# Strassen's form for 15 of 22 gate/up pairs of the first four feed-forward layers

## The chip, the cores and the metric

The kernel runs on one core of one Trainium2 chip. TensorE (PE) multiplies matrices, VectorE (DVE) and ScalarE (ACT) work on tiles elementwise, GpSimd (POOL) does elementwise work and issues some DMAs, SyncE (SP) issues most DMAs. SBUF and PSUM are the memories on the core. The metric is the device time of one execution in microseconds (us), lower being better: 3693.38 us, the median of three runs (3691.35 to 3710.01).

## The reference

One sequence of 512 tokens of width 1024, in float32, goes through two stacks of two layers each. The first stack, for each of its two layers, is

```
x = layer_norm(alpha * x + 0.5 * swiglu_ffn(x, ffn1_wi[l], ffn1_wo[l]), ...)
x = layer_norm(alpha * x + mixer(x), ...)          # even_mixer, then odd_mixer
x = layer_norm(alpha * x + 0.5 * swiglu_ffn(x, ffn2_wi[l], ffn2_wo[l]), ...)

def swiglu_ffn(x, wi, wo):                          # wi 1024 x 5632, wo 2816 x 1024
    gate, up = jnp.split(x @ wi, 2, axis=-1)
    return (jax.nn.silu(gate) * up) @ wo
```

These four `swiglu_ffn` are the feed-forward layers that the change touches. The mixers are a gated linear recurrence, an mLSTM, an RWKV and a gated linear attention. The second stack has two layers of three attention branches, each followed by a feed-forward layer with a convolution; the change leaves them alone.

## The kernel before

**Products in three parts.** Activations lie transposed, with the features in the 128 partitions and the 512 tokens in the free dimension. A float32 operand is split into a high part in float32r (`AF.Copy` to that type, on ACT) and a low part, the operand minus its high part (on DVE). `mm3` (L389) issues three matmuls for one 128 x 128 weight block: weight high by activation high, weight high by activation low, weight low by activation high. Each loads its weights anew.

**Weights.** `plan_w` lists every weight slab of the program in the order of use. A gate or up slab has 8 blocks of 128 rows by 128 columns and comes as two raw tiles `wr` of 128 x 512 (256 KB each), loaded by SP. `_split_hi` makes the high parts `wh`, `_split_lo` the low parts `wl`. `slab()` splits the slab that is now used, if that has not happened yet, and then lets `split_ahead` split `ahead` slabs more (1 in these layers), as long as no more than `hl_bufs` = 8 slabs are split and not done; `slab_done` ends a slab. `raw_bufs` = 3 slabs are loaded ahead of the splitting.

**One feed-forward layer** (`ffn_block1`, L730). The 22 blocks of 128 hidden features are done in `PARTS` of 6, 8 and 8. Each block j is a pair: a gate tile (8 blocks, 24 matmuls) and an up tile. `unit` then makes silu(gate) * 0.5 * up (`sg` on ACT, `hf` on DVE) and splits it (`hh` on ACT, `hl` on DVE). After each part, eight tiles of `wo` (`down`, `gemm_tile`) add the part to `ys`; the last part does this in `out_proj_ln`. The first two pairs of a layer are done by `gemm_first` (L555), which holds four slabs at once and loops over the eight blocks k outermost, since the layer norm before it delivers the activations block by block; in three of the four layers it does this for the two halves of the tokens one after the other. At every second k (of the second half, or of the only pass) it calls `split_ahead`. After it, eight sums `y` = `xh` + `xl` restore the activations on DVE, and pair 2 follows.

**A layer's end.** `out_proj_ln` (L685) holds its four last slabs at once and does them for each half of the tokens; the layer norm of the first half (`ln_half`, DVE and ACT) runs beside the second half's matmuls. The next stage begins with its own `gemm_first` on four slabs.

**Order.** A planner of the kernel's own (`Sched`) keeps an estimate of each engine's time while the program is written and decides where background work, such as the layer norm, stands between the main work's instructions. The framework then schedules these instructions and gives tiles their buffers; all tiles named by `g.f` share 90 buffers. DVE, ACT and POOL take their queues in order. The profile puts nearly all instructions on a helper's line (L55, L279), so tiles tell them apart: `mf` is the PSUM tile of `gemm_first`, `m` of `gemm_tile`, `mg` of `gemm_group`, `mh` of the last four slabs.

Of the kernel before, what the change touches and what calls it, by code (L numbers as in the profile page):

```python
# [12 lines left out]
F32R = mybir.dt.float32r  # L13
# [209 lines left out]
        assert not self.blocked  # L223


class G:


    def __init__(self, ctx, tc, raw_bufs=3, hl_bufs=8, f_bufs=90, q_bufs=16):
        self.s = Sched()  # L230
        self.ctx, self.tc, self.nc = ctx, tc, Core(tc.nc, self.s)
        pool = lambda name, bufs=1, **kw: ctx.enter_context(tc.tile_pool(name=name, bufs=bufs, **kw))
        self.const = pool("const")
        self.fp = pool("fp", f_bufs)
        self.qp = pool("qp", q_bufs)
        self.qsp = pool("qsp", 24)
        self.dram = pool("dram", 1, space=bass.MemoryType.DRAM)
        self.psp = pool("psp", 8, space=PSUM)
        self.raw_bufs, self.hl_bufs, self.ahead = raw_bufs, hl_bufs, 1
        self.wq = []  # L240
# [90 lines left out]
    def plan_w(self, w, c0, cols, k0, kt):  # L331

        src = w[k0 * P:(k0 + kt) * P, c0:c0 + cols].rearrange("(k p) c -> p k c", p=P)
        self.plan(lambda t, k, n: self.nc.sync.dma_start(t, src[:, k:k + n]), kt, cols)

    def _dma(self):
        while self.wi_dma < len(self.wq) and self.wi_dma < self.wi_split + self.raw_bufs:
            load, kt, cols = self.wq[self.wi_dma]
            per = NT // cols
            self.whl_t[self.wi_dma] = parts = []  # L340
            for k0 in range(0, kt, per):
                n = min(per, kt - k0)
                t = self.f("wr", F32, n * cols)
                load(t.rearrange("p (k c) -> p k c", c=cols), k0, n)
                parts.append(t)
            self.wi_dma += 1

    def split_ahead(self, n=1):

        self._dma()  # L350
        while n > 0 and self.wi_split < min(len(self.wq), self.wi_done + self.hl_bufs):
            self._split()
            n -= 1

    def _split_hi(self):
        parts = []
        for t in self.whl_t[self.wi_hi]:
            hi = self.f("wh", F32R, t.shape[1])
            self.nc.scalar.activation(hi, t, AF.Copy)
            parts.append((t, hi))  # L360
        self.whl_t[self.wi_hi] = parts
        self.wi_hi += 1

    def _split_lo(self):
        j = self.wi_split
        cols = self.wq[j][2]
        hl = []
        for raw, hi in self.whl_t[j]:
            lo = self.f("wl", F32R, raw.shape[1])
            self.nc.vector.tensor_tensor(lo, raw, hi, ALU.subtract)  # L370
            for k in range(lo.shape[1] // cols):
                c = slice(k * cols, (k + 1) * cols)
                hl.append((hi[:, c], lo[:, c]))
        self.whl_t[j] = hl
        self.wi_split += 1
        self._dma()

    def _split(self):

        if self.wi_hi == self.wi_split:  # L380
            self._split_hi()
        if self.wi_hi == self.wi_split + 1 and self.wi_hi < min(len(self.wq), self.wi_done + self.hl_bufs):
# [67 lines left out]
HALF = (slice(0, 256), slice(256, 512))  # L450
ALPHA = 4.0 ** 0.25
PARTS = ((0, 6), (6, 8), (14, 8))


class Pipe:
# [260 lines left out]
        g.s.spawn(finish(hf))  # L716


def plan_ffn(g, w_a, w_b, hook=None):
    for k0, n in PARTS:  # L720
        for j in range(k0, k0 + n):
            g.plan_w(w_a, j * P, P, 0, KD)
            g.plan_w(w_a, 2816 + j * P, P, 0, KD)
        for m in range(KD):
            g.plan_w(w_b, m * P, P, k0, n)
        if hook and k0 == 0:
            hook()


def ffn_block1(g, xs, gv, bv, hook=None, into=None, by_half=True):  # L730

    nc = g.nc
    ys = [g.f("y") for _ in range(KD)]
    st = Stats(g, True)
    pipe = Pipe()
    for pi, (k0, n) in enumerate(PARTS):
        hs = {}

        def unit(j, pg, pu):
            sg, hf = g.f("sg"), g.f("hf")  # L740
            nc.scalar.activation(sg, pg(), AF.Silu)
            g.rel()
            yield True
            nc.vector.scalar_tensor_tensor(hf, sg, 0.5, pu(), ALU.mult, ALU.mult)
            g.rel()
            hh, hl = g.f("hh", F32R), g.f("hl", F32R)
            nc.scalar.activation(hh, hf, AF.Copy)
            yield True
            nc.vector.tensor_tensor(hl, hf, hh, ALU.subtract)
            hs[j] = (hh, hl)  # L750

        j = k0
# [1899 lines left out]
def kernel(ctx: ExitStack, tc: tile.TileContext, d, out: bass.AP):  # L2652
# [25 lines left out]
    plan_ffn(g, d["ffn1_wi"][0], d["ffn1_wo"][0])  # L2678
    plan_even(g, d["ev_w_in"][0], d["ev_w_out"][0])
    plan_ffn(g, d["ffn2_wi"][0], d["ffn2_wo"][0])  # L2680
    plan_ffn(g, d["ffn1_wi"][1], d["ffn1_wo"][1])
    plan_odd(g, d["od_w_in"][0], d["od_w_out"][0], lambda l: plan_mem(g, d["w_mem_kv_2"][l]))
    plan_ffn(g, d["ffn2_wi"][1], d["ffn2_wo"][1])
    for l in range(2):
        plan_attn(g, d, l)
        plan_ffn2(g, d, l)
# [9 lines left out]
        return tc.manual_schedule(engines=e) if e != set() else contextlib.nullcontext()  # L2696

    with man("f"):
        x = ffn_block1(g, x0, *ln(0, 0), hook=lambda: g.s.spawn(first_setups()), by_half=False)
    with man("even"):  # L2700
        x = even_block(g, x, d, *ln(0, 1))
    with man("f"):
        x = ffn_block1(g, x, *ln(0, 2))
        x = ffn_block1(g, x, *ln(1, 0), hook=lambda: setup_odd(g, d))
# [50 lines left out]
```

## Time and profile before

| | us |
|---|---|
| median of 3 runs | 3693.38 (3691.35 to 3710.01) |
| the profiled execution | 3691.82 |
| its span, first to last instruction | 3689.6 |
| PE busy | 3633.5 (98%), 19704 matmuls |
| DVE busy | 2062.8 (56%) |
| ACT busy | 1460.8 (40%) |
| POOL busy | 359.2 (10%) |

The mean granted TensorE clock is 0.989 of full speed. The span holds the four changed layers at about 16 to 390, 610 to 990, 990 to 1360 and 1770 to 2140 us. An instruction's row shows its start, its duration and, in brackets, how long its engine was idle before it and what ended that; rows that are merged have a count (x2). Durations of neighbours on one engine overlap, so the distance of starts is what one costs in a dense queue.

### The profile page before, as it was taken

To read this page: it belongs to the slowest core of one execution; us is meant where nothing else is said; L and a number is where in the kernel's file an instruction comes from. 1 tells how busy PE (TensorE), PEld (TensorE's weight loads), DVE (VectorE), ACT (ScalarE), POOL (GpSimd) and SP (SyncE) were. 2 spreads that over 40 slices of the span, in tenths; PEclk is the share of its full clock that TensorE was granted. 3 is DMA by queue.
4 is the path that set the end of the run, shared out by engine and by line. 5 is a ranking of instruction groups with operands and counts; after the bars stand their busy time and mean duration, and the time that the engine had idled before them with its cause. 6 is when DMAs were issued, how large, how long until landed. Compare 5 with 4: busy or idle time off the path is not lost.

```text
span 3689.6 us, 52324 instructions
## 1 busy us (share of the span) xinstructions
PE 3633.5 (98%) x19704; PEld 2982.4 (81%) x19704; DVE 2062.8 (56%) x3771; ACT 1460.8 (40%) x2837; POOL 359.2 (10%) x547
## 2 busy tenths in 40 slices
PE   9999999999999999999999999999999999999999
PEld 7888878888888887677888888788888887888888
DVE  4333878432643266767633375557666745467755
ACT  4223664232333236534422353435333444354433
POOL 0001103000200021010100130022000300130001
PEclk9999999999999999989999999999999999999999
DMA  5333222332333221113233333332333332323231
GB/s 158 100 100 84 75 70 87 104 98 86 89 106 97 86 75 52 39 39 98 84 104 98 90 91 118 89 104 67 99 97 90 105 112 85 100 83 101 86 97 52
DMA packets 615087, 331.78 MB, mean 90 GB/s; under 512 B 25234, under 2 KB 608051, under 8 KB 614835
## 3 DMA queue, kind: packets, MB, share of 16 engines
q1 hardware_dynamic: 612018, 324.81, 30.3%
q10 hardware_dynamic: 2816, 3.64, 0.3%
q8 instruction: 154, 2.52, 0.3%
q14 instruction: 99, 0.80, 0.1%
HBM read 323.65 MB, written 4.74 MB: 89 GB/s over the span
## 4 chain that ended last, share of the span: by engine, by line
PE 91%; DVE 6%; ACT 1%; issue 1%; POOL 0%; DMA 0%; SPq 0%; DVEq 0%; POOLq 0%; ACTq 0%
PE m L279 64%; PE mg L279 5%; PE mf L279 4%; PE mh L279 4%; PE tk L279 3%; PE br L279 2%; DVE wl L55 1%; DVE ln_z L55 1%; DVE x L55 1%; DVE rm_t L55 1%; DVE rst L55 1%; PE st L279 1%; DVE xgl L55 0%; PE S L279 0%; PE mv L279 0%
## 5 line engine op out<-in xcount | busy, mean ns | idle before, releaser
L55 DVE TENSOR_TENSOR wl<-wr,wh 128x512 fp32r<-128x512 f32 (+2 forms) x1208 | 815.3, 720 | 114.9 <-ACT wh L55 114.4
L55 ACT ACTIVATE wh<-wr 128x512 fp32r<-128x512 f32 (+2 forms) x1208 | 663.9, 607 | 93.1 <-PE m L279 50.8
L279 PE MATMUL m<-xh,wh 128*128 128x512 f32 x1544 | 619.6, 401 | 0.0
L279 PE MATMUL m<-xh,wl 128*128 128x512 f32 x1544 | 610.9, 396 | 0.0
L279 PE MATMUL m<-xl,wh 128*128 128x512 f32 x1544 | 610.4, 395 | 0.0
L279 PE MATMUL m<-xgh,wh 128*128 128x512 f32 x1184 | 470.7, 398 | 0.0
L279 PE MATMUL m<-xgl,wh 128*128 128x512 f32 x1184 | 466.3, 394 | 0.0
L279 PE MATMUL m<-xgh,wl 128*128 128x512 f32 x1184 | 466.0, 394 | 0.0
L55 DVE SCALAR_TENSOR_TENSOR hf<-sg,m 128x512 f32<-128x512 f32 x80 | 55.0, 688 | 575.0 <-PE m L279 565.7
L279 PEld LDWEIGHTS m<-xh,wh 128*128 128x128 f32 x1544 | 291.0, 188 | 74.6 <-issue 7.3
L279 PEld LDWEIGHTS m<-xh,wl 128*128 128x128 f32 x1544 | 291.0, 188 | 69.1 <-issue 0.4
L279 PEld LDWEIGHTS m<-xl,wh 128*128 128x128 f32 x1544 | 291.2, 189 | 67.6 <-issue 1.7
L279 PEld LDWEIGHTS m<-xgh,wh 128*128 128x128 f32 x1184 | 222.3, 188 | 55.9 <-issue 5.3
L279 PEld LDWEIGHTS m<-xgh,wl 128*128 128x128 f32 x1184 | 222.3, 188 | 52.4
L279 PEld LDWEIGHTS m<-xgl,wh 128*128 128x128 f32 x1184 | 222.4, 188 | 49.9
L279 PE MATMUL m<-hh,wh 128*128 128x512 f32 x600 | 236.5, 394 | 0.0
L279 PE MATMUL m<-hl,wh 128*128 128x512 f32 x600 | 236.3, 394 | 0.0
L279 PE MATMUL m<-hh,wl 128*128 128x512 f32 x600 | 236.2, 394 | 0.0
L55 ACT ACTIVATE sg<-m 128x512 f32<-128x512 f32 x80 | 47.8, 598 | 424.1 <-PE m L279 424.1
L55 ACT ACTIVATE hh<-hf 128x512 fp32r<-128x512 f32 x88 | 55.7, 633 | 382.6 <-DVE hf L55 382.6
L55 ACT ACTIVATE uc<-up,vecs 128x512 f32<-128x512 f32 x88 | 71.7, 817 | 202.3 <-DVE up L55 202.3
L55 DVE SCALAR_TENSOR_TENSOR uc<-up,vecs,uc 128x512 f32<-128x512 f32 x176 | 131.3, 748 | 12.9 <-ACT uc L55 6.8
(546 smaller groups left out, 6330.3 us busy)
## 6 DMA issues: line engine op xcount, KB each, us to landing
wr<-in_ffn_wi_dram SPq DMA_DIRECT2D x352, 256.0 KB
wr<-in_w_up_dram SPq DMA_DIRECT2D x176, 256.0 KB
wr<-in_ffn_wo_dram SPq DMA_DIRECT2D x160, 256.0 KB
wr<-in_w_in_dram SPq DMA_DIRECT2D x152, 256.0 KB
wr<-in_w_down_dram SPq DMA_DIRECT2D x80, 256.0 KB
wr<-in_od_w_in_dram SPq DMA_DIRECT2D x50, 256.0 KB
wr<-in_ev_w_in_dram SPq DMA_DIRECT2D x48, 256.0 KB
wr<-in_w_out_dram SPq DMA_DIRECT2D x32, 256.0 KB
```

The lines of the kernel that those rows point to most:

```text
L55: r = fn(*a, **kw)
L279: return self.nc.tensor.matmul(out, lhsT, rhs, start=start, stop=stop, **kw)
```

## The change

Write the weights of one pair as a 2 x 2 block matrix: rows 1 and 2 are the two halves of the 1024 inputs, columns 1 and 2 are gate and up. The activations' blocks are the two halves of the inputs by the two halves of the tokens. Strassen's form (in Winograd's variant) computes gate and up with 7 block products instead of 8, of which each has 4 blocks k by 256 tokens. The names A11 to A22 are weight blocks of 128 x 512, S1 to S4 sums or differences of them, T1 to T4 those of the activations' blocks.

`FAST` names the 15 pairs that are done so: 3 to 7, 9, 10, 12 to 15, 17, 18, 20 and 21. `Combos` makes T1 to T4 and their high and low parts once per layer, spawned after the eight sums; a fast product waits for them. Each of the 7 products is a slab of one tile. Its factor is loaded or made on DVE, its high part is made on ACT; the low parts of S2 and S1 are made by a negated copy of the raw factor to float32r on ACT and a DMA from POOL's queue that adds the raw factor to it. The other five low parts are DVE's as before. `Fast.step` adds the products up, on DVE, as their PSUM banks become complete.

In the four layers, lookahead is now counted in tiles of 128 x 512: at most `RAW1` = 6 raw ones, and `HL0` = 9 (in `gemm_first` and from the last part's output on) or `HL1` = 7 (between) split and not done; `ahead` is 2.

```diff
+class Pair:
...
+    ORDER = ("A11", "S2", "A12", "S3", "S1", "A22", "S4")
+    BY_DMA = ("S2", "S1")
+    FETCH = {"A11": ("A11", "A21"), "S2": ("A22",), "A12": ("A12",)}
...
+    def factor(self, nm):
...
+        t, TT = self.t, self.g.nc.vector.tensor_tensor
+        if nm == "A11":
+            return t["A11"]
+        if nm == "S2":
+            t["S1"], t["S2"] = self.g.f("ws"), self.g.f("ws")
+            TT(t["S1"], t["A21"], t["A22"], ALU.add)
+            TT(t["S2"], t["S1"], t["A11"], ALU.subtract)
+            return t["S2"]
+        if nm == "S3":
+            TT(t["A21"], t.pop("A11"), t["A21"], ALU.subtract)
+            return t.pop("A21")
+        if nm == "S4":
+            TT(t["A12"], t["A12"], t.pop("S2"), ALU.subtract)
+            return t.pop("A12")
+        return t[nm] if nm == "A12" else t.pop(nm)
...
+    def room(self, i):
+        if i >= len(self.wq):
+            return False
+        if not self.raw_lim:
+            return i < self.wi_done + self.hl_bufs
+        return sum(1 if isinstance(load, Pair) else -(-kt * cols // NT)
+                   for load, kt, cols in self.wq[self.wi_done:i + 1]) <= self.hl_lim
+
     def split_ahead(self, n=1):
         self._dma()
-        while n > 0 and self.wi_split < min(len(self.wq), self.wi_done + self.hl_bufs):
+        while n > 0 and self.room(self.wi_split):
             self._split()
             n -= 1
...
             lo = self.f("wl", F32R, raw.shape[1])
-            self.nc.vector.tensor_tensor(lo, raw, hi, ALU.subtract)
+            if isinstance(self.wq[j][0], Pair) and self.wq[j][1] in Pair.BY_DMA:
+                self.nc.scalar.activation(lo, raw, AF.Copy, scale=-1.0)
+                self.nc.gpsimd.dma_start(lo, raw, accum_op=ALU.add)
+            else:
+                self.nc.vector.tensor_tensor(lo, raw, hi, ALU.subtract)
...
+FAST = tuple(j for j in range(3, 22) if j not in (8, 11, 16, 19))
+RAW1, HL0, HL1 = 6, 9, 7
...
+class Combos:
...
+    def make(self):
...
+        for k in range(4):
+            lo, hi = self.ys[k], self.ys[4 + k]
+            s, u = g.f("ta"), g.f("tb")
+            TT(s[:, a], lo[:, b], lo[:, a], ALU.subtract)
+            TT(s[:, b], hi[:, b], s[:, a], ALU.subtract)
+            yield g.pace()
+            TT(u[:, a], hi[:, b], lo[:, b], ALU.subtract)
+            TT(u[:, b], hi[:, a], s[:, b], ALU.subtract)
+            yield g.pace()
+            for nm, t in (("s", s), ("u", u)):
+                h, l = g.f("th", F32R), g.f("tl", F32R)
+                g.split_x(h, l, t)
...
+class Fast:
+    def product(self, nm):
...
+        w = g.slab()
+        for k in range(4):
+            x = self.cb(nm, k)
+            g.s.upto(*w[k], *x)
+            g.mm3(self.ps[bank][:, HALF[c]], w[k], x, k == 0, k == 3)
+        g.slab_done()
...
+    def step(self, nm):
...
+        self.product(nm)
...
+        if nm == "S2":
+            c = self.c1 = g.f("c1")
+            nc.scalar.copy(c[:, a], ps("a")[:, a])
+            TT(c[:, b], c[:, a], ps("a")[:, b], ALU.add)
...
+        elif nm == "S3":
+            u = self.c2 = g.f("c2")
...
+            TT(u[:, b], c[:, b], ps("b")[:, b], ALU.add)
+            TT(c[:, a], c[:, a], ps("b")[:, a], ALU.add)
...
+        elif nm == "A22":
...
+            TT(c[:, b], c[:, b], ps("d")[:, b], ALU.add)
...
+            TT(v(w), v(ps("d")), u[:, None, b].to_broadcast([P, 2, 256]), ALU.add)
...
+        elif nm == "S4":
+            c = self.c1
+            TT(c[:, b], c[:, b], ps("e")[:, a], ALU.add)
...
-def ffn_block1(g, xs, gv, bv, hook=None, into=None, by_half=True):
+def ffn_block1(g, xs, gv, bv, hook=None, into=None, by_half=True, fast=()):
     nc = g.nc
+    g.raw_lim, g.hl_lim, g.ahead = RAW1, HL0, 2
...
             for k in range(KD):
                 nc.vector.tensor_tensor(ys[k], xs.h[k], xs.l[k], ALU.add)
-        while j < k0 + n:
-            ps = [gemm_tile(g, xs)]
-            pipe.add(unit(j, lambda: ps[0], lambda: ps[1]))
-            ps.append(gemm_tile(g, xs))
-            pipe.step()
-            j += 1
+            g.hl_lim = HL1
+            cb = Combos(g, xs, ys)
+            if fast:
+                g.s.spawn(cb.make())
+        for j, nm in pair_order(range(j, k0 + n), fast):
+            if nm is None:
...
+            g.s.wait(lambda: cb.n == 4)
...
+            e.step(nm)
+            if nm == "S4":
+                pipe.add(unit_fast(j, e))
         pipe.drain()
+        if pi == len(PARTS) - 1:
+            g.hl_lim = HL0
...
+    g.raw_lim, g.ahead = 0, 1
     return xn[0]
```

## Rows read from the trace of the kernel before

**Rows 1.** The page: busy time of engines, and the chain by engine.
```profile
PE 3633.5 (98%) x19704; PEld 2982.4 (81%) x19704; DVE 2062.8 (56%) x3771; ACT 1460.8 (40%) x2837; POOL 359.2 (10%) x547
...
PE 91%; DVE 6%; ACT 1%; issue 1%; POOL 0%; DMA 0%; SPq 0%; DVEq 0%; POOLq 0%; ACTq 0%
```

**Rows 2.** The chain in order of time, whole span: start, us, engine, tile, line, count.
```profile
644.38 44.33 PE m L279 x191
697.04 114.10 PE m L279 x492
...
996.40 18.50 PE mf L279 x156
1014.90 44.50 PE m L279 x192
...
1794.94 44.55 PE m L279 x192
```

**Rows 3.** Groups by shape, PE's weight loads: busy us, mean ns, idle before.
```profile
L279 PEld LDWEIGHTS m<-xh,wh 128*128 128x128 f32 x1544 | 291.0, 188 | 74.6 <-issue 7.3
```

**Rows 4.** Timeline of DVE inside a pair of the first layer: start us, us.
```profile
151.94 1.29 DVE L55 TENSOR_TENSOR wl<-wr,wh 128x512 fp32r<-128x512 f32 x2
153.14 0.68 DVE L55 TENSOR_TENSOR hl<-hf,hh 128x512 fp32r<-128x512 f32 x1
153.74 1.29 DVE L55 TENSOR_TENSOR wl<-wr,wh 128x512 fp32r<-128x512 f32 x2
```

**Rows 5.** Groups by shape, DVE, whole span: a half-width operation on PSUM.
```profile
L55 DVE TENSOR_TENSOR y<-y,mh 128x256 f32<-128x256 f32 x48 | 19.9, 415 | 21.0 <-PE mh L279 21.0
```

**Rows 6.** Timeline of ACT inside a pair of the first layer.
```profile
130.39 1.14 ACT L55 ACTIVATE wh<-wr 128x512 fp32r<-128x512 f32 x2
```

**Rows 7.** Waits of PE: in total, times, longest, us.
```profile
PE xT L284 <- DMA xs<-in_x_dram: 7.9, 7, 3.7
```

**Rows 8.** Timeline of DVE after the third layer's `gemm_first`.
```profile
1015.85 0.69 DVE L55 SCALAR_TENSOR_TENSOR hf<-sg,mf 128x512 f32<-128x512 f32 x1 [3.40 <-ACT sg L55]
1017.23 0.69 DVE L55 TENSOR_TENSOR hl<-hf,hh 128x512 fp32r<-128x512 f32 x1 [0.70 <-ACT hh L55]
...
1018.44 4.90 DVE L55 TENSOR_TENSOR y<-xh,xl 128x512 f32<-128x512 f32 x8
1023.26 1.28 DVE L55 TENSOR_TENSOR wl<-wr,wh 128x512 fp32r<-128x512 f32 x2
```

**Rows 9.** Timeline of PE: first product of pair 2, first layer.
```profile
38.84 0.40 PE L279 MATMUL m<-xh,wh 128*128 128x512 f32 x1
```

**Rows 10.** Timeline of DVE: first wl behind the sums, layers 1, 2 and 4.
```profile
52.00 1.29 DVE L55 TENSOR_TENSOR wl<-wr,wh 128x512 fp32r<-128x512 f32 x2
...
651.40 1.29 DVE L55 TENSOR_TENSOR wl<-wr,wh 128x512 fp32r<-128x512 f32 x2
...
1802.39 1.29 DVE L55 TENSOR_TENSOR wl<-wr,wh 128x512 fp32r<-128x512 f32 x2
```

**Rows 11.** Timeline of DVE between the second and the third layer.
```profile
995.16 0.43 DVE L55 TENSOR_TENSOR sq<-sq,sqt 128x256 f32<-128x256 f32 x1
...
997.42 1.30 DVE L55 TENSOR_TENSOR wl<-wr,wh 128x512 fp32r<-128x512 f32 x2
998.63 0.42 DVE L55 TENSOR_TENSOR rst<-st_v,rs 128x256 f32<-128x256 f32 x1
```

**Rows 12.** Windows of 2 us: busy us of each engine, granted clock, DMA share, GB/s.
```profile
570.00:572.00 2.00, 1.42 (x7) 0.81 (x5) 2.00 (x2) 0.00 (x0) 2.00 (x3) 1.00 0.78 220
572.00:574.00 2.00, 0.28 (x1) 0.31 (x2) 1.49 (x4) 0.88 (x3) 2.00 (x3) 0.88 0.14 43
574.00:576.00 2.00, 2.00 (x6) 1.52 (x6) 0.78 (x3) 1.74 (x2) 0.46 (x2) 0.50 0.01 4
576.00:578.00 2.00, 2.00 (x11) 1.74 (x10) 1.72 (x3) 0.18 (x1) 0.00 (x0) 0.76 0.00 0
```

More of the change, by code (lines that the diff above doesn't have):

```diff
@@ L223, in drain, with __init__, fetch @@
         assert not self.blocked
+class Pair:
+    ORDER = ("A11", "S2", "A12", "S3", "S1", "A22", "S4")
+    BY_DMA = ("S2", "S1")
+    FETCH = {"A11": ("A11", "A21"), "S2": ("A22",), "A12": ("A12",)}
+    def __init__(self, g, w, c1, c2):
+        self.g, self.t = g, {}
+        self.src = {n: w[512 * (b - 1):512 * b, c:c + P].rearrange("(k p) c -> p k c", p=P)
+                    for n, b, c in (("A11", 1, c1), ("A12", 2, c1), ("A21", 1, c2), ("A22", 2, c2))}
+    def fetch(self, nm):
+        for n in self.FETCH.get(nm, ()):
+            t = self.t[n] = self.g.f("wr")
+            self.g.nc.sync.dma_start(t.rearrange("p (k c) -> p k c", c=P), self.src[n])
+    def factor(self, nm):
[14 more added lines that the diff above has]
+        return t[nm] if nm == "A12" else t.pop(nm)
 class G:
@@ L334, in plan_w, with raw_tiles @@
         self.plan(lambda t, k, n: self.nc.sync.dma_start(t, src[:, k:k + n]), kt, cols)
+    def raw_tiles(self, a, b):
+        n = 0
+        for load, kt, cols in self.wq[a:b]:
+            n += len(Pair.FETCH.get(kt, ())) if isinstance(load, Pair) else -(-kt * cols // NT)
+        return n
     def _dma(self):
-        while self.wi_dma < len(self.wq) and self.wi_dma < self.wi_split + self.raw_bufs:
+        while self.wi_dma < len(self.wq) and (
+                self.raw_tiles(self.wi_split, self.wi_dma) < self.raw_lim if self.raw_lim else
+                self.wi_dma < self.wi_split + self.raw_bufs):
             load, kt, cols = self.wq[self.wi_dma]
+            if isinstance(load, Pair):
+                load.fetch(kt)
+                self.whl_t[self.wi_dma] = None
+                self.wi_dma += 1
+                continue
             per = NT // cols
@@ L356, in _split_hi @@
         parts = []
+        load, nm, _ = self.wq[self.wi_hi]
+        if isinstance(load, Pair):
+            self.whl_t[self.wi_hi] = [load.factor(nm)]
         for t in self.whl_t[self.wi_hi]:
@@ L716, in out_proj_ln, with pair_order, plan_ffn @@
         g.s.spawn(finish(hf))
-def plan_ffn(g, w_a, w_b, hook=None):
-    for k0, n in PARTS:
-        for j in range(k0, k0 + n):
-            g.plan_w(w_a, j * P, P, 0, KD)
-            g.plan_w(w_a, 2816 + j * P, P, 0, KD)
+def pair_order(js, fast):
+    for j in js:
+        for nm in Pair.ORDER if j in fast else (None,):
+            yield j, nm
+def plan_ffn(g, w_a, w_b, hook=None, fast=()):
+    for k0, n in PARTS:
+        pairs = {}
+        for j, nm in pair_order(range(k0, k0 + n), fast):
+            if nm is None:
+                g.plan_w(w_a, j * P, P, 0, KD)
+                g.plan_w(w_a, 2816 + j * P, P, 0, KD)
+            else:
+                if j not in pairs:
+                    pairs[j] = Pair(g, w_a, j * P, 2816 + j * P)
+                g.plan(pairs[j], nm, P)
         for m in range(KD):
@@ L727, in plan_ffn, with __init__, __call__ @@
             hook()
-def ffn_block1(g, xs, gv, bv, hook=None, into=None, by_half=True):
+class Combos:
+    def __init__(self, g, xs, ys):
+        self.g, self.xs, self.ys = g, xs, ys
+        self.t = {}
+        self.n = 0
+    def make(self):
+        g = self.g
+        TT = g.nc.vector.tensor_tensor
+        a, b = HALF
+        for k in range(4):
[10 more added lines that the diff above has]
+                g.split_x(h, l, t)
+                self.t[nm, k] = (h, l)
+            self.n = k + 1
+            yield g.pace()
+        self.ys = None
+    PLACE = {"T1": ("s", 0), "T2": ("s", 1), "T3": ("u", 0), "T4": ("u", 1)}
+    OF = {"A11": "B11", "A12": "B21", "S4": "B22", "A22": "T4", "S1": "T1", "S2": "T2", "S3": "T3"}
+    def __call__(self, nm, k):
+        b = self.OF[nm]
+        if b[0] == "B":
+            return self.xs(k + 4 * (int(b[1]) - 1), HALF[int(b[2]) - 1])
+        o, q = self.PLACE[b]
+        h, l = self.t[o, k]
+        return h[:, HALF[q]], l[:, HALF[q]]
@@ new lines, with __init__ @@
+class Fast:
+    PLACE = {"A11": ("a", 0), "S2": ("a", 1), "A12": ("b", 0), "S3": ("b", 1), "S1": ("d", 1), "A22": ("d", 0),
+             "S4": ("e", 0)}
+    def __init__(self, g, cb):
+        self.g, self.cb = g, cb
+        self.ps = {}
+    def product(self, nm):
+        g = self.g
+        bank, c = self.PLACE[nm]
+        if bank not in self.ps:
+            g.acq_main(1)
+            self.ps[bank] = g.psum("m")
+        w = g.slab()
[4 more added lines that the diff above has]
+        g.slab_done()
+        g.s.pump()
+    def step(self, nm):
+        g, nc, TT = self.g, self.g.nc, self.g.nc.vector.tensor_tensor
+        self.product(nm)
+        ps = self.ps.get
+        a, b = HALF
+        if nm == "S2":
+            c = self.c1 = g.f("c1")
+            nc.scalar.copy(c[:, a], ps("a")[:, a])
+            TT(c[:, b], c[:, a], ps("a")[:, b], ALU.add)
+            del self.ps["a"]
+            g.rel()
+        elif nm == "S3":
[3 more added lines that the diff above has]
+            TT(c[:, a], c[:, a], ps("b")[:, a], ALU.add)
+            del self.ps["b"]
+            g.rel()
+        elif nm == "A22":
+            u, c = self.c2, self.c1
+            TT(c[:, b], c[:, b], ps("d")[:, b], ALU.add)
+            v = lambda t: t.rearrange("p (h n) -> p h n", h=2)
+            w = g.f("c2")
+            TT(v(w), v(ps("d")), u[:, None, b].to_broadcast([P, 2, 256]), ALU.add)
+            self.c2 = w
+            del self.ps["d"]
+            g.rel()
+        elif nm == "S4":
+            c = self.c1
+            TT(c[:, b], c[:, b], ps("e")[:, a], ALU.add)
+            del self.ps["e"]
+            g.rel()
@@ L750, in unit, with unit_fast @@
             hs[j] = (hh, hl)
+        def unit_fast(j, e):
+            sg, hf = e.c1, e.c2
+            nc.scalar.activation(sg, sg, AF.Silu)
+            yield True
+            nc.vector.scalar_tensor_tensor(hf, sg, 0.5, hf, ALU.mult, ALU.mult)
+            hh, hl = g.f("hh", F32R), g.f("hl", F32R)
+            nc.scalar.activation(hh, hf, AF.Copy)
+            yield True
+            nc.vector.tensor_tensor(hl, hf, hh, ALU.subtract)
+            hs[j] = (hh, hl)
         j = k0
@@ L760, in ffn_block1 @@
                 nc.vector.tensor_tensor(ys[k], xs.h[k], xs.l[k], ALU.add)
-        while j < k0 + n:
-            ps = [gemm_tile(g, xs)]
-            pipe.add(unit(j, lambda: ps[0], lambda: ps[1]))
-            ps.append(gemm_tile(g, xs))
-            pipe.step()
-            j += 1
+            g.hl_lim = HL1
+            cb = Combos(g, xs, ys)
+            if fast:
+                g.s.spawn(cb.make())
+        open_ = {}
+        for j, nm in pair_order(range(j, k0 + n), fast):
+            if nm is None:
+                ps = [gemm_tile(g, xs)]
+                pipe.add(unit(j, lambda: ps[0], lambda: ps[1]))
+                ps.append(gemm_tile(g, xs))
+                pipe.step()
+                continue
+            g.s.wait(lambda: cb.n == 4)
+            if j not in open_:
+                open_[j] = Fast(g, cb)
+            e = open_[j]
+            e.step(nm)
+            if nm == "S4":
+                pipe.add(unit_fast(j, e))
+                del open_[j]
         pipe.drain()
+        if pi == len(PARTS) - 1:
+            g.hl_lim = HL0
         of = lambda k, c=slice(0, NT): (hs[k0 + k][0][:, c], hs[k0 + k][1][:, c])
@@ L2702 @@
     with man("f"):
-        x = ffn_block1(g, x, *ln(0, 2))
-        x = ffn_block1(g, x, *ln(1, 0), hook=lambda: setup_odd(g, d))
+        x = ffn_block1(g, x, *ln(0, 2), fast=FAST)
+        x = ffn_block1(g, x, *ln(1, 0), hook=lambda: setup_odd(g, d), fast=FAST)
     mkv, mhl = [], ([], [])
@@ L2711 @@
         rx = ffn_block1(g, x, *ln(1, 2),
-                            into=lambda: RX(g, [g.f("x") for _ in range(KD)], v["g_pre_mix0"]))
+                            into=lambda: RX(g, [g.f("x") for _ in range(KD)], v["g_pre_mix0"]), fast=FAST)
     for l in range(2):
```

13 lines of the change are left out of this document (7 added, 6 removed).

## The prediction

> **What bounds the kernel now.** I read the page first: its first part gives TensorE (PE) 98% of the span and VectorE (DVE) 56%, and the chain that ended last is PE work for 91% [rows 1]. So time leaves only with PE work, or comes where PE is made to wait. The chain in order of time then gives both prices of a product. A stretch of 492 products, all with 512 moving columns (16 gate/up tiles of 24 and 6 down tiles of 18), takes 114.10 us: 0.2319 each. 156 products with 256 columns take 18.50 us: 0.1186 each [rows 2]. Halving the columns costs only 2% per column, though each product loads new weights.
>
> Last, I read the joints between stages, where the chain leaves PE, in the timelines of DVE and PE; their rows come with the parts below that use them.
>
> **Products removed.** An ordinary pair is 2 tiles x 8 k x 3 = 48 products: 48 x 0.2319 = 11.13 us. A fast pair is 7 block products x 4 k x 3 = 84 products of 256 columns: 84 x 0.1186 = 9.96 us. Four layers x 15 pairs x 1.17 us = **70 us saved**, all on PE's path.
>
> Each fast pair also loads weights 84 times instead of 48. A load's row is 188 ns [rows 3], longer than the 0.1186 us step, yet products with a load each keep that step [rows 2]; so the loads lie under products, and I add nothing. [...]
>
> **DVE in a fast pair.** Back to back, full-width operations start 0.60 us apart (two wl at 151.94, hl at 153.14, wl at 153.74) [rows 4]. A half-width one shows 0.415 [rows 5] where a full one shows 0.68; I take 0.33 apart. Factors: 4 subtractions or additions. Low parts: 5 (two of seven go to DMAs). 9 x 0.60 = 5.4. Evacuation: five half-width and one full: 2.25. The unit's hf and hl: 1.2. Sum 8.85 us against 9.96 of PE; before it was 3.6 (four low parts, hf, hl) against 11.13. ACT: 7 high parts, 2 negated copies, one half copy, silu, hh at about 0.52 apart (two wh in 1.14 [rows 6]): 5.9 us. So a fast pair stays PE-bound if nothing waits: cost 0. The upper bound: with the window of 7 tiles full, each split writes factor, high part, low part in a row, so at S3 and S4 DVE also waits for ACT, some 0.75 us each: 10.35 us per pair, 0.4 x 60 = 24 us. I keep 0, since an ordinary pair (3.6 of 11.13) stands after every second or third fast one and the window is some 6 products deep.
>
> **The adding DMAs.** No row of before shows one. S2's low part is written when product A12 of the pair before starts, and is needed 6 products later, 6 x 1.42 + 0.24 = 8.8 us. Evacuating S2 (1.0), the two additions (1.3), high part and negated copy (1.3) come first; 5.1 us are left. The nearest row is a plain load of the same 256 KB: PE's longest wait for the first input tile is 3.7 us from the start of the program [rows 7]. Below 5.1 it is hidden: 0 (and no gain, as the DVE time saved is counted above). Were it 6 us, S2 would wait 0.9 in every pair: 54 us. [...]
>
> **The new wait at each layer's start.** HL0 = 9 counts tiles of 512 columns. `gemm_first` holds four slabs of two tiles, 8, until its last product; the next slab would make 10. So its four `split_ahead` calls do nothing, where before they prepared four slabs. The gate slab of pair 2 is now split only in its own `slab()` call. That stands behind hf, hl, hf and the eight sums y = xh + xl in DVE's queue, and DVE keeps the written order: before, it waits 0.70 us for hh at 1017.23, though the sums' inputs are long there [rows 8]. The first low part therefore lands where now the first wl behind the sums ends, 1023.26 + 0.69 = 1023.95; PE is free at 1014.90 and has two products (0.46) that need no low part: 8.6 us idle. In the same way (52.00, 651.40 and 1802.39 against 38.84, 644.38 and 1794.94 [rows 2, 9, 10]): 13.4, 7.2 and 7.7. **37 us** for four layers. Bounds: 18 if the sums were passed by (4 x 4.8 less), 37 as the queue stands.
>
> **The sums of activations.** Combos add 16 half-width operations (0.36 apart, as half of them need the one before) and 8 low parts: 10.6 us on DVE, 11.6 with the waits for ACT's high parts. From the end of the eight sums DVE also does gate, up and A11 low parts (3.0), S1 and S2 (1.25), hl and hf of pair 2 (1.2), A12's low part and S3 (1.2): 18.25 less the last low part, 17.6 until product S2 has its fourth operand. PE gets there in 0.69 + 10.7 + 1.42 + 1.07 = 13.9. [...] I take 3.5: **14 us**; bounds 0 and 6 per layer. Queued behind on DVE are the low parts of S3 and A22; S1's DMA is issued only then, and S1 is due about 3 us later: 0 to 2 us, I take 1: **4 us**.
>
> **The new wait at each layer's end.** The four last slabs of `out_proj_ln` are again 8 of 9 tiles, so the next stage's first four slabs are no longer prepared there. They are split at the next `gemm_first`: 8 high and 8 low parts, behind the last sq (995.16 to 995.59) [rows 11]. Low part 1 is ready at 996.3, the seventh, needed by the fourth tile's first product, at 999.9; the first 12 products end at 1000.3, and then 84 more half-width products of the first half follow: 1010.2, and 96 of the second: 1021.6 against 1014.90 [rows 2]. 6.7 us; at least 4.8, the 8 x 0.60 that DVE gains in a stretch where it has almost no idle time (the layer norm). I take 6: **24 us**.
>
> [...]
>
> **Sum.** -70 + 37 + 14 + 4 + 24 = +9 us on the profiled execution's 3691.82 (span 3689.6 and 2.2 around it): 3700.8. It lies 1.6 below the median of the runs, so I predict **3702 us**, no change: this kernel's measurement can't tell less than about 0.5% (18 us).
>
> **Rivals.** (1) *Faster*: the splits pass the sums. Speaks for it: in the layer norm, wl instructions stand between its operations (997.42, before rst) [rows 11], so something fills gaps; against it: the 0.70 us wait above. Then the first wait is 18, the one at the end 2 each: -70 + 18 + 14 + 4 + 8 = -26: 3667. (2) *Slower*: DVE becomes the engine that sets a fast pair's time. For: 8.85 of 9.96 leaves 1.1 us, and the two factor-to-low-part waits are 1.5. Against: the ordinary pairs between. It decides once DVE needs over 9.96 per pair; at 10.6 (0.25 more for waits on PE's evacuations) it is 0.65 x 60 = 39 us more: 3741; a late adding DMA gives much the same (54). (3) The half-width products don't run at 0.1186 in this order: with 0.188 per load they take 15.8 us a pair, 4.7 x 60 = 280 more than before: 3974. Against it: the 156 products of [rows 2].
>
> **Chances.** Forecast 0.50, of it 0.08 above the bound of slower; (1) 0.22, of it 0.02 within the bound; (2) 0.25; (3) 0.03. Faster by over 0.5%: 0.20; within: 0.44; slower: 0.36. The range reaches from (1) to (2): 3662 to 3745; the forecast's own, by the bounds of the first wait, the sums and the end, is 3680 to 3720.
>
> **What would show it.** PE m products of 256 columns at 0.118 apart, 5040 of them. Per layer one PE wait of 7 to 13 us for wl just after mf, one of some 4 us for the first tl, and 5 us of waits on wh or wl before the next stage's mf. In pairs 6 to 21 no PE wait of note, DVE busy near 90%. PE waiting there for DVE or for a wl that a DMA wrote proves (2); no wait before pair 2 proves (1); the prediction is wrong if either moves more than 18 us.

## The result, and the profile after

The changed kernel takes 3720.97 us (median of 6 runs, 3713.64 to 3725.79), the kernel before 3696.23 beside it (6 runs, 3691.35 to 3710.01). The ratio is 1.0058 [1.0039, 1.0077]: slower by 0.6%. The forecast was 3702 and "no change"; the time lies 19 us above it, inside the range (3662 to 3745), and the slowdown, small as it is, is clear of the noise. The profiled execution took 3724.09 (span 3722.3), 32.3 more than the one before, where the medians differ by 24.7: the profiled execution of the kernel before is one of its shortest.

The page after, beside [rows 1]: PE has 34.7 us less to do, yet the span is longer, and PE's share of the chain that ended last falls from 91 to 86%. DVE, ACT, a DMA and issue took that share.

```profile
PE 3598.8 (97%) x21864; PEld 3060.2 (82%) x21864; DVE 2435.4 (65%) x4527; ACT 1664.1 (45%) x3230; POOL 453.4 (12%) x667
...
PE 86%; DVE 8%; ACT 2%; issue 2%; DMA 1%; POOL 0%; SPq 0%; DVEq 0%; ACTq 0%; POOLq 0%
```

The chain in order of time, third layer after (start, us, engine, tile, line, count), which answers to [rows 2]:

```profile
1010.38 22.36 PE mf L319 x183
...
1040.88 0.61 DVE wl L55
1041.54 7.29 PE m L319 x22
1048.92 0.60 ACT sg L55
...
1061.59 4.40 DMA wl<-ws
1066.03 22.97 PE m L319 x192
1088.99 8.33 PE mg L319 x36
1097.33 106.81 PE m L319 x708
1204.13 11.09 PE mg L319 x48
1215.22 115.35 PE m L319 x744
1330.58 11.14 PE mg L319 x48
```

Three things are to be seen. Of the 192 products of `gemm_first` (mf) 183 lie on the chain, for 156 before, since none of them now runs ahead of the layer norm's end. Behind them PE stands until 1041.54, but for two products at 1037.3, and from 1048.92 on the chain hops over ACT, DVE and a DMA until 1066.03. From there PE alone is the chain: mg to mg takes 115.14 and 126.45 us in parts 2 and 3 of the layer, where the kernel before took 122.43 and 133.54. So steady state won and the joints lost.

Waits of PE after (total us, times, longest), which answers to [rows 7]. The tile st is the layer norm's statistics, which PE makes from the tiles sum and sq; th and tl are the high and low parts of T1 to T4, ws the factors S1 and S2. Before, sum was 3.7 and sq 1.1; the other four did not exist:

```profile
PE m L319 <- ACT wh L55: 18.4, 4, 5.1
PE st L319 <- DVE sum L55: 18.1, 5, 4.7
PE m L319 <- DVE wl L55: 12.5, 8, 3.5
...
PE st L319 <- DVE sq L55: 7.6, 2, 6.4
PE m L319 <- ACT th L55: 5.9, 5, 1.8
PE m L319 <- DMA wl<-ws: 5.5, 8, 1.6
```

Of the 12.5 us for wl 10.5 stand in front of pair 2, with the 18.4 for wh; PE's own rows show both in the third layer, 3.5 us each. The last mf product starts at 1033.50.

```profile
1037.30 0.50 PE L319 MATMUL m<-xh,wh 128*128 128x512 f32 x1 [3.52 <-ACT wh L55]
...
1041.54 0.80 PE L319 MATMUL m<-xh,wl 128*128 128x512 f32 x1 [3.51 <-DVE wl L55]
```

The timeline of DVE behind the third layer's `gemm_first`, after, which answers to [rows 8]: the same hf, hl, hf and eight sums, and the first low part behind them; only now PE needs that one.

```profile
1033.39 0.69 DVE L55 SCALAR_TENSOR_TENSOR hf<-sg,mf 128x512 f32<-128x512 f32 x1 [7.87 <-ACT sg L55]
1034.77 0.69 DVE L55 TENSOR_TENSOR hl<-hf,hh 128x512 fp32r<-128x512 f32 x1 [0.69 <-ACT hh L55]
1035.38 0.68 DVE L55 SCALAR_TENSOR_TENSOR hf<-sg,mf 128x512 f32<-128x512 f32 x1
1035.98 4.90 DVE L55 TENSOR_TENSOR y<-xh,xl 128x512 f32<-128x512 f32 x8
1040.80 3.10 DVE L55 TENSOR_TENSOR wl<-wr,wh 128x512 fp32r<-128x512 f32 x5
```

Windows of 2 us there (columns as in [rows 12]; the granted clock is the third number from the right). PE was idle from 1034 on, but for those two products; the granted clock falls to 0.73 and 0.50, and is still 0.50 and 0.56 in the two windows after PE resumes at 1041.54:

```profile
1034.00:1036.00 2.00, 0.00 (x0) 0.00 (x0) 1.31 (x4) 1.11 (x2) 0.00 (x0) 1.00 0.00 0
...
1038.00:1040.00 2.00, 0.03 (x1) 0.00 (x0) 2.00 (x4) 1.33 (x3) 0.00 (x0) 0.73 0.00 0
1040.00:1042.00 2.00, 0.46 (x1) 0.46 (x2) 2.00 (x4) 0.00 (x0) 0.00 (x0) 0.50 0.00 0
1042.00:1044.00 2.00, 2.00 (x6) 1.52 (x6) 2.00 (x5) 0.00 (x0) 0.00 (x0) 0.50 0.00 0
1044.00:1046.00 2.00, 2.00 (x7) 1.57 (x6) 1.97 (x4) 0.63 (x1) 0.00 (x0) 0.56 0.00 0
```

### The profile page after: what moved, and what is told of

Its sections match the earlier page's. It is cut to its first block, busy times and chain, and to the rows that moved or that the text cites. A ratio compares the mean times of both kernels' runs of the same rounds, so it can differ in the third digit from the quotient of the medians.

```text
span 3722.3 us, 58449 instructions
## 1 busy us (share of the span) xinstructions
PE 3598.8 (97%) x21864; PEld 3060.2 (82%) x21864; DVE 2435.4 (65%) x4527; ACT 1664.1 (45%) x3230; POOL 453.4 (12%) x667
## 4 chain that ended last, share of the span: by engine, by line
PE 86%; DVE 8%; ACT 2%; issue 2%; DMA 1%; POOL 0%; SPq 0%; DVEq 0%; ACTq 0%; POOLq 0%
PE m L319 59%; PE mg L319 5%; PE mf L319 4%; PE mh L319 4%; PE tk L319 3%; PE br L319 2%; DVE wl L55 1%; DMA wl<-ws 1%; DVE x L55 1%; DVE ln_z L55 1%; DVE rm_t L55 1%; DVE y L55 1%; PE st L319 1%; DVE xgl L55 1%; DVE rst L55 0%
## 5 line engine op out<-in xcount | busy, mean ns | idle before, releaser
L55 DVE TENSOR_TENSOR wl<-wr,wh 128x512 fp32r<-128x512 f32 (+1 forms) x1268 | 854.7, 712 | 261.3 <-ACT wh L55 237.9
L55 ACT ACTIVATE wh<-wr 128x512 fp32r<-128x512 f32 (+1 forms) x1268 | 698.4, 608 | 120.1 <-PE m L319 48.3
L319 PE MATMUL m<-xh,wh 128*128 128x256 f32 (+1 forms) x1304 | 450.1, 345 | 18.4 <-ACT wh L55 18.4
L319 PE MATMUL m<-xh,wl 128*128 128x256 f32 (+1 forms) x1304 | 441.4, 339 | 10.5 <-DVE wl L55 10.5
L319 PE MATMUL m<-xl,wh 128*128 128x256 f32 (+1 forms) x1304 | 440.2, 338 | 0.0
L319 PE MATMUL m<-th,wl 128*128 128x256 f32 x960 | 272.0, 283 | 7.6 <-DMA wl<-ws 5.5
L319 PE MATMUL m<-th,wh 128*128 128x256 f32 x960 | 271.0, 282 | 5.9 <-ACT th L55 5.9
L319 PE MATMUL m<-tl,wh 128*128 128x256 f32 x960 | 270.5, 282 | 1.7 <-DVE tl L55 1.7
L55 POOL DMA_DIRECT2D wl<-ws x120 | 103.4, 861 | 1158.5 <-ACT wl L55 835.6
L319 PEld LDWEIGHTS m<-th,wl 128*128 128x128 f32 x960 | 181.7, 189 | 10.6 <-DMA wl<-ws 7.7
```

Of the source, the lines that this page charges most:

```text
L55: r = fn(*a, **kw)
L319: return self.nc.tensor.matmul(out, lhsT, rhs, start=start, stop=stop, **kw)
```

## The experiments

Theory: the products win their 70 us, and the lookahead limit of 9 tiles (no room to prepare slabs at a layer's start and end), the sums of activations and the adding DMA at the first fast pair give back more. Rivals: DVE sets a fast pair's time, or the adding DMAs are late throughout.

A ratio is to the kernel before, timed beside it. For each kernel the table also gives what the layers' starts cost: the time from the last product of `gemm_first` to the first mg, read in the four layers' timelines of PE (before: 45.7, 44.4, 44.6, 44.6). The loss is their sum, less 179.3 for the kernel before, plus 1.17 for each fast pair in that stretch (12 in all where pair 3 is the first fast one, 8 where pair 4 is, none in e4). It is read from one profile of each kernel; kernels whose starts are the same program (the change and e3, e1 and e2, e5 and e8) agree within 1.5 us.

| kernel | median, us | ratio [95%] | four starts | loss there |
|---|---|---|---|---|
| before | 3696 to 3704 | 1 | 179.3 | 0 |
| the change | 3720.97 | 1.0058 [1.0039, 1.0077] | 230.3 | 65 |
| e4_no_fast | 3759.81 | 1.0147 [1.0129, 1.0164] | 221.4 | 42 |
| e3_end17 | 3690.85 | 0.9967 [0.9947, 0.9987] | 231.7 | 66 |
| e2_start17 | 3699.84 | 0.9986 [0.9973, 0.9998] | 207.3 | 42 |
| e1_both17 | 3674.00 | 0.9922 [0.9899, 0.9944] | 207.6 | 42 |
| e10_lim9_from4 | 3697.32 | 0.9987 [0.9974, 1.0001] | 213.1 | 43 |
| e12_sums_later | 3705.72 | 1.0010 [0.9996, 1.0025] | 211.8 | 42 |
| e11_lim9_dve | 3713.35 | 1.0036 [1.0020, 1.0052] | 221.8 | 57 |
| e6_s1_dve | 3671.41 | 0.9929 [0.9900, 0.9958] | 213.3 | 48 |
| e7_all_dve | 3659.09 | 0.9880 [0.9846, 0.9914] | 201.7 | 36 |
| e5_from4 | 3643.30 | 0.9839 [0.9809, 0.9869] | 184.0 | 14 |
| e8_18pairs | 3630.59 | 0.9808 [0.9778, 0.9837] | 184.3 | 14 |
| e9_18_dve | 3626.33 | 0.9793 [0.9770, 0.9817] | 181.9 | 12 |

**The limit.**

```diff
-RAW1, HL0, HL1 = 6, 9, 7
+RAW1, HL0, HL1 = 6, 17, 7            # e1: both; e2 and e3 put 17 in one of its two places
-FAST = tuple(j for j in range(3, 22) if j not in (8, 11, 16, 19))
+FAST = ()                            # e4: the lookahead alone, HL0 = 9
```

> HL0 = 17 instead of 9: gemm_first and out_proj_ln hold their 8 tiles and may prepare four more slabs, as the kernel before did. Theory (the limit of 9 tiles makes the waits): pair 2's gate has its low parts when mf ends (no PE wait there), the next stage's four slabs are ready (no 5 to 7 us at each end). DVE must still make the sums, so product S2 of pair 3 keeps waiting for the last tl, some 8 us per layer instead of 14. Against the changed kernel about -30 at the starts and -24 to -34 at the ends: 3655 to 3665 us, 35 under the kernel before. Rival (DVE is full in the fast pairs, the waits only move): within 10 us of the changed kernel, 3711 or more.

> Only the layers' starts get 17 tiles; the ends keep 9. Theory: PE's waits for wh and wl before pair 2 (31 us in four layers) go, those for sum and sq at the ends (26 us) stay; 20 to 35 us under the changed kernel: 3686 to 3700. Rival (DVE full): no change, 3715 or more.

> Only the layers' ends get 17 tiles; the starts keep 9. Theory: the four joints after the layers come back to the 48 us of the kernel before from 53 to 55 (24 us in all), and the mixers behind them, which are 10 us longer in the changed kernel, come back too if they only suffer from the late start: 3685 to 3697. Rival (the mixers' 10 us have another cause): 3695 to 3700 with the mixers still longer.

> No pair is fast (and so no sums of activations are made), but the changed lookahead stays (6, 9 and 7 tiles, ahead 2). Theory: all four starts wait for wl as in the changed kernel (8 to 13 us each, 37), all four ends too (24), mixers 10: 60 to 75 us over the kernel before, 3755 to 3770; the 84-product pairs then save 70 less what the sums cost. Rival (the losses at the starts belong to the fast pairs' DVE work, not to the limit): only the ends, 3715 to 3730.

The new lookahead alone costs 1.47%, or 54 us (e4). That is its three limits and the deeper `ahead` together; that HL0 makes most of it is shown by e1, which raises HL0 alone at both places, is 47 us faster than the change, and beats the kernel before by 0.8%. e2, e3 and e4 came inside their ranges, e1 did not (3674 for 3655 to 3665): its starts keep a loss of 42 us, over 10 a layer for the 8 expected. Each place takes its own waits with it, as PE's waits show, in e4, in e3 (ends raised) and in e2 (starts raised), in that order:

```profile
PE m L319 <- ACT wh L55: 18.4, 4, 5.1
PE st L319 <- DVE sum L55: 18.0, 5, 4.9
PE m L319 <- DVE wl L55: 10.0, 4, 3.0
PE st L319 <- DVE sq L55: 7.9, 4, 6.1
```
```profile
PE m L319 <- ACT wh L55: 19.8, 4, 5.1
PE m L319 <- DVE wl L55: 12.0, 8, 3.0
```
```profile
PE st L319 <- DVE sum L55: 17.9, 5, 4.7
PE m L319 <- ACT th L55: 13.5, 14, 2.9
...
PE st L319 <- DVE sq L55: 7.5, 2, 6.4
```

But e2 wins 23 of the starts' 65 us, not 37: with the parts of pair 2 in time, PE now waits for th 13.5 us, where it was 5.9. e4 gives the price of the first wait alone. In its third layer the last mf product ends at 1051.98, and the first product that needs a low part starts at 1059.73; PE's rows book 6.5 us of that as idle. Then 190 products take 46.90 us, which at 0.2319 are 44.06. The 2.8 us between are the lower clock: the granted clock is 0.50 up to 1064 us and 0.66 in the 2 us behind.

```profile
1059.07 0.61 DVE wl L55
...
1059.73 46.90 PE m L319 x190
```
```profile
1062.00:1064.00 2.00, 2.00 (x6) 1.58 (x5) 1.29 (x3) 0.00 (x0) 0.00 (x0) 0.50 0.10 28
1064.00:1066.00 2.00, 2.00 (x7) 1.55 (x7) 0.00 (x0) 0.00 (x0) 0.00 (x0) 0.66 0.45 131
```

**The first fast pair.** What is left at the starts should be pair 3 standing too close behind the sums.

```diff
-FAST = tuple(j for j in range(3, 22) if j not in (8, 11, 16, 19))
+FAST = tuple(j for j in range(4, 22) if j not in (8, 13, 18))     # e5 with HL0 = 17, e10 with 9
```

> Both limits at 17 (as e1_both17), and the 15 fast pairs are 4 to 21 without 8, 13 and 18, so that a second ordinary pair (11.13 us) stands between gemm_first and the first fast pair. Theory: in e1_both17 part 0 of a layer still loses some 9 us (50.2 in the second layer, against 44.33 - 3.5 = 40.8), because pair 3 follows the sums too closely: DVE makes T1 to T4 while pair 3's products wait for th (2.8 us), its S1 for the low part that a DMA writes (2.0), and the clock is down for 3.4 us behind these. With one more ordinary pair between, this work lies under it: 8 us less in each of four layers, 32 in all: ratio to before 0.992 - 0.0087 = 0.983 (3642 against 3704), waits of PE for th and for wl written by DMA under 3 us each. Rival: DVE is late by its total work in the first two pairs, and the same waits come back at pair 4: ratio 0.990 to 0.994.

> The change as it is (limit 9), but the 15 fast pairs are 4 to 21 without 8, 13 and 18. Theory: of the change's loss at a layer's start, what the sums and S1's late low part cost is there only because pair 3 is the first fast pair; with one ordinary pair more it goes, as it went from e1_both17 to e5_from4 (0.992 to 0.984). The 8.6 us wait for pair 2's first low part stays, and so do the ends. So 25 to 31 us under the change's 1.0058: ratio 0.997 to 0.999. Rival: with limit 9 DVE is behind by another 8 us, the same waits come back at pair 4 and little is won: 1.002 to 1.006.

Both times came as the theory had them: 0.9922 to 0.9839 with limit 17, 1.0058 to 0.9987 with limit 9. The loss at the starts falls from 42 to 14 and from 65 to 43. The 43 of e10 are the 42 of e4: with one more ordinary pair between, and the wait in front of it, sums and DMA cost nothing more. In e5, without that wait, they are not wholly hidden: PE's wait for th is 1.1 us as expected, but the one for low parts by DMA is 8.6, where under 3 were expected.

In e10 the wait for pair 2's low part remains; e12 asks whether it is only the order of DVE's queue.

```diff
+            g.hl_lim = HL1
+            g.split_ahead(2)
             for k in range(KD):
                 nc.vector.tensor_tensor(ys[k], xs.h[k], xs.l[k], ALU.add)
-            g.hl_lim = HL1
```

> e10_lim9_from4 with the eight sums y = xh + xl written behind the splits of pair 2's two slabs. Theory: what PE waits for behind gemm_first is its first low part, and this stands behind the sums only by the written order. The high parts of pair 2 come at once behind hh in ACT's queue (at 1036.64 in the third layer of the change), so the first low part lands some 3.8 us sooner (1037.7 for 1041.5): four layers: 15 us: ratio to before 0.9987 - 0.004 = 0.9946, and PE's waits m <- wh and wl, now 18.4 + 10.5, fall to 12 to 16. Rival: DVE's whole work before the first fast pair sets the end, not its order: the wait at pair 2 falls, but th or c are late at pair 4 by as much, and the ratio stays at 0.998 to 0.999.

The order did what it should, for the low part. In the third layer the second hf starts 3.82 us later than in e10 (1023.17 against 1019.35) and the first low part only 0.29 later, so 3.5 us sooner by the layer's own time, and PE's wait on wl, 10.5 us in e10, is down to 0.2 a layer. The larger wait, for the high parts (18.4 in e10), stays at 17.0, and the low part itself now stands behind its high part:

```profile
1023.17 0.68 DVE L55 SCALAR_TENSOR_TENSOR hf<-sg,mf 128x512 f32<-128x512 f32 x1
1025.06 2.50 DVE L55 TENSOR_TENSOR wl<-wr,wh 128x512 fp32r<-128x512 f32 x4 [1.22 <-ACT wh L55]
1027.48 4.90 DVE L55 TENSOR_TENSOR y<-xh,xl 128x512 f32<-128x512 f32 x8
```

No time came of it: the loss at the starts is 42 for 43, and the ratio is 1.0010 for 0.9987. Of the 11 us that PE no longer waits in front of pair 2, 7 come back as waits at the first fast pairs: the one for low parts written by DMA goes to 8.3 us from 2.0 (whole span), the one for th to 1.2 from none. Waits of PE in e10, then in e12:

```profile
PE m L319 <- DVE wl L55: 10.5, 4, 3.5
```
```profile
PE m L319 <- ACT wh L55: 17.0, 4, 4.9
PE m L319 <- DMA wl<-ws: 8.3, 7, 2.8
```

So the rival holds in the main: DVE's whole backlog before the first fast pair sets the end (in e12's third layer its queue has some 5 us of idle time from 1025 to 1062), and a wait taken from its front comes back at its end. Where the other 3 us went, the waits do not show. (Of the 8 us between the medians the starts show none; in the profiles e12 is 5 us longer between the third and the fourth layer, where the clock varies, as told in the last section.)

**The adding DMAs, and DVE's room.**

```diff
-    BY_DMA = ("S2", "S1")
+    BY_DMA = ()                      # e11 with HL0 = 9, e7 with 17; e6: ("S2",)
```

> The change as it is (limit 9, fast pairs from 3), without adding DMAs: DVE makes the low parts of S1 and S2 too. Theory: the DMAs cost only at the first fast pair of a layer, where S1's low part lands 4.4 us after its issue and PE waits 5.5 us in all, with the clock down behind: 5 to 15 us less than the change: ratio 1.002 to 1.0045. Rival A (DMAs are hidden, DVE is short of room): 0.6 to 1.2 us more of DVE in each fast pair, 10 us or more slower than the change: 1.0085 or above. Rival B: no difference, 1.005 to 1.0065.

> Both limits at 17; S1's low part is made by DVE, S2's alone by an adding DMA. Theory (DVE is the engine with room, the DMA's landing late only at a layer's first fast pair): the wait of PE for wl written by DMA (6.6 us in e1_both17, all on S1) goes, DVE's backlog there grows by 0.6, and other pairs hide the 0.6 of DVE (windows of fast pairs show DVE busy 0.80 to 0.88): ratio to e1_both17 0.998 to 1.000, 0 to 7 us faster. Rival (a fast pair is near DVE's bound, the DMA is what keeps it on PE): 45 pairs behind another fast pair lose 0.3 us or more each: 14 us slower or more.

> Both limits at 17; both low parts are made by DVE, no adding DMA at all. By my estimate DVE then needs 8.85 + 1.2 = 10.05 us for a fast pair of 9.96. Theory (DVE has room, as ordinary pairs stand between): within 8 us of e6_s1_dve, waits of PE for DVE's c or wl under 8 us in all. Rival (DVE becomes the bound, the second rival of the prediction): 60 pairs x 0.3 to 0.6 = 18 to 36 us slower than e1_both17.

Without DMAs the loss at the starts falls by 8.5 us (e11) and 6 (e7), and the medians by 8 and 15, though their intervals overlap those of the kernels with DMAs; e11's ratio lies in the range of its theory. In e6 the wait for low parts by DMA stayed at 7.3 us: PE now waits for S2's, which is issued behind the same backlog, and the starts lose 6 more; its time is that of e1. The theory that only S1's is late was wrong; taking one DMA away is no cure. e7 is 12 us faster than e6, where I expected them within 8. No kernel showed the rival, DVE as the bound. The hardest test takes the ordinary pairs away from e5:

```diff
-FAST = tuple(j for j in range(4, 22) if j not in (8, 13, 18))
+FAST = tuple(range(4, 22))           # e8 with BY_DMA as in the change, e9 with ()
```

> Both limits at 17; all 18 pairs from 4 to 21 are fast, with no ordinary pair between. Beside e5_from4 it has 3 x 4 = 12 more fast pairs. Theory (a fast pair is bound by PE, 8.85 us of DVE under 9.96): 12 x 1.17 = 14 us faster than e5_from4. Rival (DVE catches up only in the ordinary pairs): no faster than e5_from4, or slower, with PE waiting for wl or for DVE's evacuation (a bank of c) in the last pairs of each run of fast ones.

> Both limits at 17, pairs 4 to 21 all fast (as e8_18pairs), and no adding DMA: DVE makes every low part. In e8_18pairs PE waits 9.9 us for low parts that DMAs write, the largest wait left in the fast pairs. Theory (DVE has no room for nine full-width operations more than it has where fast pairs follow each other: by my estimate 10.05 us for 9.96): the 9.9 us go, but DVE falls behind in runs of eight fast pairs, so no faster than e8_18pairs: ratio to before 0.979 to 0.988. Rival (DVE has room even then): 10 us faster than e8_18pairs: 0.976 to 0.979, with waits of PE for wl, c or m under 4 us in all.

e8 is 12.7 us faster than e5 (14 expected). e9 is no slower than e8, so the theory written for it, that DVE falls behind in runs of fast pairs, is wrong: its ratio, 0.9793, is at the edge between the two expectations, and the DMA waits are gone. Windows of the eight fast pairs that follow each other in the second layer, of e8 and then of e9 (length, busy us of PE, PEld, DVE, ACT, POOL, then the clock):

```profile
708.40:788.10 79.70, 79.70 (x673) 79.56 (x672) 67.47 (x127) 47.63 (x90) 12.01 (x14) 1.00 0.63 149
```
```profile
705.40:784.80 79.40, 79.40 (x673) 79.40 (x672) 74.57 (x139) 40.12 (x76) 0.00 (x0) 1.00 0.34 100
```

PE is busy throughout in both. DVE is busy 8.43 us of a pair's 9.96 in e8 and 9.32 of 9.93 in e9: it has room even when it makes all low parts, but only 0.6 us a pair. e9, with limit 17, 18 fast pairs from pair 4 and no DMA, is the best version: 2.07% [1.83, 2.30] faster than the kernel before.

## Why the prediction was right, and where its sizes were off

The forecast was built as a gain of 70 against losses of 79. Both are there, and the sum came within 24 us of the profile's 32.3. In part that is luck: the wait at the starts was put 9 us too high, the loss of 14 behind it, mostly lower clock, has no term in the sum, and the two all but cancel. By the profiles, whose terms add up to 33 where the medians differ by 24.7:

| term | predicted | measured |
|---|---|---|
| products | -70 | -70 |
| wait at each layer's start | 37 | 28.4 (e4) |
| loss behind that wait, mostly lower clock | no term | 13.6 (e4: 42.0 less the wait) |
| sums of activations | 14 | 14.5 (what is left) |
| S1's adding DMA | 4 | 8.5 (e11) |
| layers' ends | 24 | 33 |
| rest, 3 of it in the odd mixer | 0 | about 5 |

**Products.** The 48 fast pairs of parts 2 and 3 save 55.7 us in the four layers (from the first mg to mh, 278.3 before; 264.8, 263.9, 263.9 and 264.9 after): 1.16 each, for 1.17. The other 12 stand in part 1, which hides them; I count them at 1.17. The step of 0.1186 per half-width product held, each with a load of its own: in e9's window above the 672 products of eight pairs take 79.40 us, 0.1182 each, and PE and its loads are both busy for all of it. So the loads lie under the products, as forecast, and don't add their 0.188 to each, as rival (3) has it.

**The start.** The step was right in its place and in its mechanism, the split that comes only with pair 2's own `slab()` call. PE waits 6.1, 7.9, 7.0 and 7.9 us in the four layers (wh and wl together, 28.9) for the 13.4, 7.2, 8.6 and 7.7 predicted. Three are near. The first was misread: in the kernel before the row at 52.00 is late for another reason, ACT's three table loads for other work, of 1.28 us each, behind which the second sg starts at 45.94; in the change the second hf starts at 40.94 and the first low part at 46.43. Also, 18.4 of the 28.9 us are booked to the high part, which the prediction did not name. What failed is that the forecast's sum has no term for a lower clock behind that wait. In e4, where no fast pair follows and DVE has no sums of activations to make, 13.6 us of the starts' loss are no wait, and 10.5 of these lie in the 190 products behind it, which take 47.03, 45.81, 46.90 and 47.01 us in the four layers for 44.06 each (in the third at granted clocks of 0.50 and 0.66, as told above). The bound "18 if the sums were passed by" was no bound on time: e12 passed them by and won nothing.

**Sums and DMA.** What the change loses at the starts beyond e4 is 23 us, predicted 18. e11 puts 8.5 of it on the DMAs, and 14.5 is left for the sums; 3 us of this are lower clock in the first layer, where the granted clock is 0.50 from 70 to 76 us (in the other three it is 1.00 throughout the first fast pair). The mis-sized term is the DMA: I gave it 0 to 2 us per layer, since S1 is due 3 us after its issue. In the third layer it was issued at 1061.59 and landed 4.40 later, and PE waited 1.58 for it. In the four starts PE waits 4.8 us for low parts by DMA, near the 4 predicted; what makes the rest of the 8.5 was not separated. The median of all 120 is 4.0 us from issue to landing (last number of the row), under the 5.1 that a pair leaves:

```profile
wl<-ws POOLq DMA_DIRECT2D x120, 256.0 KB, 4.0
```

So inside the layer they are hidden, as forecast, but with little to spare: in the first and the fourth layer the chain runs over four of them, of 4.72 to 4.95 us, and PE waits 0.7 us there in all.

**The ends.** From mh to the next stage the kernel before took 233.7 (first layer, to the end of the even mixer), 47.6 (second) and 387.7 us (fourth, to the mh at 2505.51 in the second stack); after, 247.1, 53.5 and 394.3. With 6.9 at the third layer's joint that is 33. I had named the wrong wait. I let PE wait for low parts inside the next `gemm_first`; it waits before st (18.1 us for sum, 7.6 for sq, up to 6.4 at once). In the kernel before the first half of the next mf stood there: its first product ran 4.8 us ahead of the last sq (995.16 [rows 11]), while the second half's layer norm was still on DVE:

```profile
990.36 0.28 PE L279 MATMUL mf<-xh,wh 128*128 128x256 f32 x1
```

Without prepared slabs these products can't fill that place. The size of that, "at least 4.8", was near for three of the four; the stretch behind the first layer lost 13.4, and 4.0 of it is a wait inside the even mixer that the prediction did not have:

```profile
PE num L319 <- DVE E L55: 4.0, 1, 4.0
```

The kernel before does not show that wait, nor does e3 with the ends raised, whose first stretch is back at 233.6 us; with the limit and no fast pair (e4) it is 244.4. How the limit reaches that far into the mixer was not followed up.

**Signs.** The 5040 half-width products are there. The wait behind mf came as 6 to 8 us a layer, half or more of it for wh; the one for the first tl as 1.3 to 1.8 us for th and 0.3 for tl at a time, not 4; the one at the ends before st. From pair 6 on PE waits 0.7 us in four layers. The forecast's own range, 3680 to 3720, doesn't come out of its bounds at the lower end (all three at their lowest give 3664); the measured time is just past the upper one.

**Rivals.** (1) is refuted: the sums were not passed by, and passing them, tried with pair 4 as the first fast one, did not pay. (2) is refuted by e7 and e9, but it was not far: DVE needs 8.43 us of a pair in e8 (8.85 predicted) and 9.32 with all low parts, of 9.96. (3) is refuted above. The chance of slower by over 0.5% (0.36) is the case that came, just past the bound: the forecast's own case with losses larger than it had.

## What to carry to other kernels

A change of the arithmetic came with a change of the lookahead, and the lookahead cost 54 us by the medians (68 by the two profiled executions), against the 70 that the products save; look at what a limit in a new unit lets through at each joint. Price a wait of PE together with the lower clock behind it: in e4 28 us of waiting cost 42, and in its third layer the granted clock was 0.50 for the first 4 us behind the wait. As e10 and e12 show, a joint's cost can be set by all the work that is queued on the helper engine until the next place with slack, so that taking one wait from its front moves the time to its end; put the new form one ordinary unit later instead (e5: 31 us for a list of numbers). Before moving work to a DMA to spare an engine, see whether the engine is short at all.

## What the runs showed of the hardware that was not expected

The clock in the odd mixer varies from one execution to the next, where instructions and waits are nearly the same (PE's waits there are 13.9 us in e9 and 12.9 in e7). The stretch from the third layer's last output to the mixer's took 401.0 us before, and 400.4 in e9 but 418.3 in e7. Windows of 50 us at the same place, e9 and then e7 (the granted clock is the third number from the right):

```profile
1483.08:1533.08 50.00, 48.03 (x542) 34.34 (x542) 30.04 (x54) 19.32 (x31) 0.10 (x1) 0.86 0.13 33
```
```profile
1510.41:1560.41 50.00, 48.03 (x464) 35.11 (x463) 25.99 (x44) 15.78 (x25) 0.10 (x1) 0.63 0.12 33
```

PE is busy for the same 48.03 us in both, but at 0.63 it does 464 products instead of 542. These 18 us are nearly the spread of the kernel before (3688 to 3710). So the spans of single profiles here can't be compared to better than some 18 us; stretches of them can. What makes the clock of one execution differ from that of the next was not tried and stays open.
